# Moving five pieces of a hybrid decoder layer by a step: coupling, inversion's head, TT's second copy, the compressed weights, and the first scores' fill

## The chip, the cores and the metric

The kernel runs on one core of a Trainium2 chip. The metric is the device time of one execution in microseconds (us), as the median of several runs. Beside it stands one profiled execution, from which all the rows come.

## The reference, cut to what matters

One decoder layer with 512 tokens and a model width of 1024, in float32. A normalised stream goes through one input projection and feeds two mixers: RWKV-7 time mixing (16 heads of 64) and native sparse attention (16 heads of 64 in 4 groups; a compressed, a selected and a sliding-window branch, each a softmax). Both are gated and merged, projected and added; a gated MLP with a causal convolution of width 3 follows.

```python
def step(state, inp):                       # RWKV-7, per head, state 64 x 64
    sa = einsum('bhvk,bhk->bhv', state, a_t)
    state = state * w_t + sa[..., None] * b_t + v_t[..., None] * k_t
    return state, einsum('bhvk,bhk->bhv', state, r_t)

k_cmp = compress(kc, ...)                   # gelu(blocks of 32 tokens @ w1) @ w2
v_cmp = compress(vc, ...)
p_c = masked_softmax(q @ k_cmp - alibi); o_c = p_c @ v_cmp
o_s = softmax over the selected blocks;  o_w = softmax over the window
out = g0 * o_c + g1 * o_s + g2 * o_w

m = sigmoid(z_a) * (o_a @ w_branch_rwkv) + sigmoid(z_b) * (o_b @ w_branch_nsa)
x = x + rms_norm(m @ w_out)
x = x + rms_norm((silu(conv(h @ up_gate)) * conv(h @ up_val)) @ down)
```

## The kernel before

Each product in full precision is made of three matmuls: weights and stream are split into a high and a low part (`wh`, `wl`, `hh`, `hl`). The split of a weight block is a load on the SP queue, a cast on ACT (L124, tiles named `...h`) and a subtraction on POOL (L162, tiles named `...l`). `proj_steps` (L302 to L309) makes one block of 128 outputs in 8 steps of three matmuls (L306, L307, L308), and gives the turn away after each step. These steps are the *fill*: work that TensorE (PE) can always do, and beside which the dependent chains run.

The rest is written as generators. `drive(fill, *threads)` gives turns: in every turn each thread first advances by its rate (0.6 means three steps in five turns) and then the fill by one step. A `yield` in a generator is thus a unit of distance in the program's order. The program's order isn't yet that of the engines: a planner orders each engine's instructions when the program is built. It plays the program with modelled times and issues, on each engine, the earliest instruction of the program that it believes ready; `tc.keep_in_program_order` and `behind` (behind the last registered eviction on the same engine) pin single ones. On the chip, an engine works through its list in order and waits at an instruction whose inputs are late.

RWKV-7 is done in chunks of 64 tokens, for 8 pairs of heads in two groups of four (`GP` = 4). For each pair `p`:

- `inputs(p)`: three blocks of projections (K, R, V), 24 fill steps.
- `prep(p)`: decays and scaled keys on ACT, DVE and POOL. Its last products are `KB` and, on DVE at L576, the row block `AR`.
- `couple(p)`: copies of Dc, then some yields (L595), the turning of V on PE (`pv`, from L597) and the products of `KB` with `AR` on PE (`g`, L611), their masks on DVE (GS, L614), stores of the chunks' triangles (`ld`, `l2`, SP queue), the turning of `KB` (`pt`), its copies to BKT, the products LV and a bonus that is stored to `bvd`.

The drive of a pair runs `prep(p)` and `couple(p)` as one thread with rate `PR` = 0.6 beside the next pair's inputs as fill. In front of pair 0, `compress(kv)` makes the compressed keys (kv = 0) and values (kv = 1) as a thread of rate 0.8: 16 matmuls (`hid`), a chain for the gelu on DVE and ACT (tiles `hu`, `hv`, L416 to L427), two yields, and the last product (`kcm`; for the values at L441).

For each group, `invert` inverts the triangles of 32 x 32: loads of XL (SP queue), two yields, a copy to XP on ACT (L661), sixty operations in a row on DVE (L666, L668), then `ID` yields to the load of x1, and up to `IE` yields to a copy, two transposes and the first parts of TT. `recur`, a thread that starts `RD` = 67 turns later, makes the second triangle's block by two rounds of products (`mt`, L709; `mm`, L733) with evictions on ACT and DVE; between the rounds ACT copies the diagonal parts to TT (L722 to L724, one copy for each half of the partitions). After that come the eight chunks of the recursion, which read TT (L810) from the first on.

In the attention, `score(p8)` makes the scores of a pair of heads in 8 steps: products on PE (`s`, L1093 and L1100), a subtraction with minimum on DVE (L1107), the exponential on ACT (L1109), and the norming on DVE and POOL (L1083, L1081); `compressed(p8)` runs inside it and leaves its normed weights in `sc` (POOL, L1055). `values(p8)` has five steps, in which PE turns those weights (`turned(k)`, L140, tiles `pt`) and multiplies them with the values (`products(k)`, L1156). The compressed weights are turned to `pct` (PE, copy on ACT at L1129, low part on DVE at L1130) in the first of these steps, and read in the third:

```python
for x in range(2):
    te.matmul(acc, vcp[:, g, x, :], pct, start=x == 0, stop=False)      # L1176
```

This product opens the accumulation to which all others of the value are added. One value's steps, the next pair's scores and some fill steps (6 to 10, `FILL2`) are sorted into one order by hand. In front of value 0, `score0` runs the first scores alone with two fill steps for each of the eight; the value with index 3 (`PX`) takes what is left of this fill (`rest`) and begins with the next one, the branch products (`ub`).

Of the kernel before, what the change touches and what calls it, by code (L numbers as in the profile page):

```python
# [31 lines left out]
WS = (1, 2, 3, 3)  # L32
GP = 4
PR, CR, IY, FR = 0.6, 0.5, 31, 0.5
ID, IE, RD, RR, NG0, NQ1, PX, FN = (30, 30), (54, 54), (67, 67), (1.05, 0.85), 8, 4, 3, 1.15
NW, NU, PA, SK = 13, 3, 0.25, 4
GRP = (((0, 2), (1, 2)), ((0, 1), (0, 3)), ((0, 0),), ((1, 1), (1, 3)), ((1, 0),))
ONACT, FILL2 = (0, 2, 4, 6, 7, 8), (9, 9, 9, 6, 10, 10, 10, 10)
# [4 lines left out]
def hybrid_layer(ctx: ExitStack, tc: tile.TileContext, a, out, dbg=None, stop=None):  # L43
# [33 lines left out]
    def pz(name):  # L77
        return pzs[-1][1].tile([128, 512], F32, tag="pz", name=name, bufs=2)
# [325 lines left out]
    def compress(kv):  # L404
        w1 = cp.tile([128, 16, 128], F32, tag="w1", name=f"w1{kv}", bufs=2)
        sy.dma_start(w1, a["w1k" if kv == 0 else "w1v"])
        w2 = cp.tile([128, 64], F32, tag="w2", name=f"w2{kv}", bufs=2)
        sy.dma_start(w2, a["w2k" if kv == 0 else "w2v"])
        ph = pz(f"hid{kv}")
        for l in range(16):  # L410
            te.matmul(ph[:, 0:129], w1[:, l, :], KCs[kv][:, l % 8, l // 8:l // 8 + 129], start=l == 0, stop=l == 15)
            if l % 8 == 7:
                yield
                yield
        hb = cp.tile([128, 1], F32, tag="hb", name=f"hb{kv}", bufs=2)
        ve.tensor_copy(hb, ph[:, 0:1])  # L416
        u = cp.tile([128, 4, 32], F32, tag="hu", name=f"hu{kv}", bufs=2)
        w = cp.tile([128, 4, 32], F32, tag="hv", name=f"hv{kv}", bufs=2)
        po.memset(u, 0.0)
        ve.tensor_scalar(u[:, :, 0:NCMP], ph[:, 2:130].rearrange("p (g n) -> p g n", n=32)[:, :, 0:NCMP], hb, None,  # L420
                         op0=OP.add)
        ve.tensor_tensor(w, u, u, op=OP.mult)
        ve.tensor_scalar(w, w, 0.044715, 1.0, op0=OP.mult, op1=OP.add)
        ve.tensor_tensor(w, w, u, op=OP.mult)
        sc.activation(w, w, AF.Tanh, scale=float(np.sqrt(2.0 / np.pi)))
        ve.tensor_scalar(w, w, 0.5, 0.5, op0=OP.mult, op1=OP.add)
        ve.tensor_tensor(u, u, w, op=OP.mult)  # L427
        yield
        yield
        pm = pz(f"kcm{kv}")  # L430
        if kv == 0:
            te.matmul(pm[0:64, 0:128], w2, u.rearrange("p g n -> p (g n)"), start=True, stop=True)
            k4 = pm[0:64, 0:128].rearrange("p (g n) -> p g n", n=32)
            sc.activation(kcs[0:64, :, 0], k4, AF.Copy)
            ve.tensor_tensor(kcs[0:64, :, 1], k4, kcs[0:64, :, 0].bitcast(F32), op=OP.subtract)
            sy.dma_start(kcs[64:128].bitcast(F32), kcs[0:64].bitcast(F32))
        else:
            for e in range(2):
                es = slice(e * 32, e * 32 + 32)
                for g in range(4):  # L440
                    te.matmul(pm[es, g * 64:g * 64 + 64], u[:, g, :], w2, start=True, stop=True)  # L441
            for q in (0, 64):
                sc.activation(vcc[q:q + 64], pm[0:64, 0:256].rearrange("p (g d) -> p g d", d=64), AF.Copy)
# [143 lines left out]
    def couple(p, o, gr, i):  # L587
        R, VW, Q, EC, KB = o.R, o.VW, o.Q, o.EC, o.KB
        AR = gr.AR[i]

        if Q is not None:
            sc.activation(AR[:, 0, :], Q, AF.Copy)
        po.tensor_tensor(AR[:, 1, :].rearrange(c8, t=64), R.rearrange(c8, t=64), EC[:, :, 1:65], op=OP.mult)
        sc.activation(gr.Dc[:, i], EC[:, :, 64], AF.Copy)
        for _ in range(3 if i == GP - 1 else 2):  # L595
            yield
        for q in range(2):  # L597
            pv = px(f"pv{p}{q}")
            for j in range(4):
                c = 4 * q + j  # L600
                tr(pv[:, j * 128:(j + 1) * 128], VW[:, c * 64:c * 64 + 128], ident)
            pvv = pv.rearrange("p (c h f) -> p c h f", h=2, f=64)
            sc.activation(gr.UV[64:128, 4 * q:4 * q + 4, i], pvv[64:128], AF.Copy)
        m4 = mask.rearrange("p (s t) -> p s t", t=64)[:, None].to_broadcast([128, 4, 2, 64])
        for q in range(2):
            gh = [(pz, py)[q](f"g{p}{q}{h}") for h in range(2)]
            for j in range(4):
                c = 4 * q + j
                for h in range(2):
                    hs = slice(h * 64, (h + 1) * 64)  # L610
                    te.matmul(gh[h][:, j * 128:(j + 1) * 128], KB[hs, c].rearrange("p s t -> p (s t)"),  # L611
                              AR[hs, :, c * 64:(c + 1) * 64], start=True, stop=True)
            for h in range(2):
                ve.tensor_tensor(gr.GS[:, 0:2 + i:1 + i, 4 * q:4 * q + 4, h].rearrange("p s c t -> p c s t"),  # L614
                                 gh[h].rearrange("p (c s t) -> p c s t", s=2, t=64), m4, op=OP.mult)
            po.tensor_tensor(KB[:, 4 * q:4 * q + 4].rearrange("p c s t -> p c (s t)"),
                             KB[:, 4 * q:4 * q + 4].rearrange("p c s t -> p c (s t)"),
                             EC[:, 4 * q:4 * q + 4, 64:65].to_broadcast([128, 4, 128]), op=OP.mult)
        yield
        yield  # L620
        for b in range(2):
            bs = slice(b * 32, (b + 1) * 32)
            sy.dma_start(gr.ld[b, i].rearrange("c h i t -> i (c h) t"), gr.GS[bs, 0, :, :, bs])
        sy.dma_start(gr.l2[i].rearrange("c h i t -> i (c h) t"), gr.GS[0:32, 0, :, :, 32:64])
        yield
        yield
        pt = [px(f"pt{p}{q}") for q in range(2)]
        for q in range(2):
            for j in range(4):
                c = 4 * q + j  # L630
                m = tr(pt[q][:, j * 128:(j + 1) * 128], KB[:, c].rearrange("p s t -> p (s t)"), ident)
                if c == 0:
                    tc.keep_in_program_order(m)
            sc.activation(gr.BKT[i][:, 4 * q:4 * q + 4, :], pt[q].rearrange("p (c f) -> p c f", f=128), AF.Copy)
        pl = py(f"pl{p}")
        for c in range(8):
            for h in range(2):
                te.matmul(pl[h * 64:(h + 1) * 64, c * 64:(c + 1) * 64], gr.GS[64:128, 0, c, h, :],
                          gr.UV[64:128, c, i, h, :], start=True, stop=True)
        sc.activation(gr.LV[:, i], pl.rearrange(c8, t=64), AF.Copy)  # L640
        pbo = py(f"pbo{p}")
        te.matmul(pbo, onesr, o.rbh, start=True, stop=False)
        te.matmul(pbo, onesr, o.rbl, start=False, stop=True)
        bv = rw.tile([128, S], F32, tag="T", name=f"bv{p}", bufs=NT)
        ve.tensor_tensor(bv, pbo, VW[:, 64:], op=OP.mult)
        sy.dma_start(bvd[p], bv)
        yield
        yield

    def invert(gr, g):  # L650
        XL = rh_.tile([128, 2, 32, 32], F32, tag="XB", name=f"XL{g}", bufs=2)
        LU, XU = XL[:, 0], XL[:, 1]
        TM = rh_.tile([128, 256], F32, tag="TM", name=f"TM{g}", bufs=1)
# [40 lines left out]
    def recur(gr, g):  # L694
# [24 lines left out]
                else:  # L719
                    ve.tensor_copy(M2[up, 2 * q:2 * q + 2], ptv[up])  # L720
        evict(act_m)
        for h in range(2):  # L722
            lo = slice(64 * h, 64 * h + 32)
            behind(sc.activation(gr.diag[0][lo, :, 0:32], gr.diag[1][lo], AF.Copy))  # L724
        yield
        for q in range(GP // 2):
            pm = px(f"mm{g}{q}")
            pmv = pm.rearrange(gi, i=2, j=32)
            for i in range(2):
# [4 lines left out]
                                  stop=True)  # L734
                yield
                yield
            for h in range(2):
                lo = slice(64 * h, 64 * h + 32)
                if h == 0:
                    sc.activation(TT[lo, 2 * q:2 * q + 2, :, 32:64], pmv[lo], AF.Copy)  # L740
                else:
                    ve.tensor_copy(TT[lo, 2 * q:2 * q + 2, :, 32:64], pmv[lo])
# [378 lines left out]

    def values(p8, o):
        g = p8 // 2
        pt = pz(f"pct{p8}")
        acc = pz(f"o{p8}")
        for qb in range(4):
            tr(pt[0:64, qb * 128:(qb + 1) * 128], o.s[:, 2 * qb:2 * qb + 2].rearrange("p h n -> p (h n)"), ident)
        pct = nw.tile([128, S], F32R, tag="pct", name=f"pct{p8}", bufs=1)
        sc.activation(pct[0:64], pt[0:64], AF.Copy)  # L1129
        ve.tensor_tensor(pct[64:128], pt[0:64], pct[0:64].bitcast(F32), op=OP.subtract)  # L1130
        PTs = []

        def turned(k):
            m, parts = [], []
# [35 lines left out]
            behind_next.pop()()  # L1170
        yield
        turned(1)
        yield
        turned(2)
        for x in range(2):
# [55 lines left out]

    def score0():
        for i, _ in enumerate(score(0, os_[0])):
            for _ in range(2):
                next(fill, None)
            yield

# [361 lines left out]
```

## Time and profile before

| What | us |
|---|---|
| runs | 1161.18, 1160.72, 1158.92; median 1160.72 |
| the profiled execution | 1158.86 |
| its span | 1157.1 |
| TensorE (PE) busy | 1136.9 |
| weight loads of TensorE (PEld) busy | 912.6 |
| DVE, ACT, POOL busy | 585.2, 588.2, 555.8 |

PE's clock was granted in full (0.998 over the execution). In a row of a timeline the columns are start, length, engine, line, operation, out<-in with shapes, and in brackets how long the engine stood idle before it and what ended this. PEld is the loading of weights, which overlaps the matmuls. A matmul's end is modelled, so its length is longer than the distance to the next one. In a list of waits, PE stood at the first name until the second one's instruction was done.

### The profile page before, as it was taken

What the parts mean: (1) busy time and instruction counts of PE and PEld (TensorE: products, weight loads), DVE (VectorE), ACT (ScalarE), POOL (GpSimd) and SP (SyncE); (2) the same over time, 40 slices, a digit from 0 to 9 for tenths busy, and PEclk for the clock granted to TensorE, in tenths of its full rate; (3) what the DMA queues carried; (4) which work ended last, traced back from release to release, by engine and by line L of the source; (5) the groups of instructions that cost most, each with busy time, mean ns of one, the idle gap of its engine ahead of it and who ended that gap; (6) DMA issues with size and microseconds to landing.
All of it is one profiled execution on the core that took longest, in us unless ns stands there. A gap on an engine that the chain in (4) does not pass through costs nothing.

```text
span 1157.1 us, 19755 instructions
## 1 busy us (share of the span) xinstructions
PE 1136.9 (98%) x7338; PEld 912.6 (79%) x7338; DVE 585.2 (51%) x1194; ACT 588.2 (51%) x1158; POOL 555.8 (48%) x530
## 2 busy tenths in 40 slices
PE   9999999999999999999999999999999999999997
PEld 7888887877888787666677778889888888888886
DVE  4246655735665643677798745654333333331103
ACT  6447673544666334576676644444444444443311
POOL 4345654435765443466454425401566565564440
PEclk9999999999999999999999999999999999999999
DMA  7422345322433753125452136631233333334421
GB/s 262 108 77 80 96 108 167 103 83 64 130 107 107 201 180 111 57 81 151 145 164 67 56 108 198 221 113 47 84 99 94 98 100 93 100 100 137 127 64 73
DMA packets 95507, 131.95 MB, mean 114 GB/s; under 512 B 34033, under 2 KB 36913, under 8 KB 95154
## 3 DMA queue, kind: packets, MB, share of 16 engines
q1 hardware_dynamic: 79490, 116.26, 32.9%
q10 hardware_dynamic: 15920, 14.42, 4.1%
q8 instruction: 58, 0.95, 0.4%
q14 instruction: 39, 0.32, 0.1%
HBM read 108.30 MB, written 19.14 MB: 110 GB/s over the span
## 4 chain that ended last, share of the span: by engine, by line
PE 52%; DVE 1%; POOL 1%; issue 0%; ACT 0%; DVEq 0%; POOLq 0%; ACTq 0%
PE pu L222 6%; PE pu L223 6%; PE pu L221 6%; PE dn L1330 3%; PE dn L1329 3%; PE dn L1331 3%; PE o L1156 3%; PE ub L1213 3%; PE ub L1214 2%; PE ub L1215 2%; PE pt L140 2%; PE s L1100 1%; PE wo L1403 1%; PE wo L1401 1%; PE wo L1402 1%; PE s L1093 1%
## 5 line engine op out<-in xcount | busy, mean ns | idle before, releaser
L1109 ACT ACTIVATE p<-p,stt 128x384 f32<-128x384 f32 (+3 forms) x128 | 70.7, 554 | 33.6 <-DVE stt L1107 32.0
L1471 DVE SCALAR_TENSOR_TENSOR u<-pu,cvec,u 128x511 f32<-128x511 f32 x44 | 33.0, 750 | 101.0 <-ACT u L1470 101.0
L1107 DVE CUSTOM_DVE_ANT_0 p<-s,rh 128x384 f32<-128x384 f32 (+3 forms) x128 | 59.2, 484 | 23.6 <-PE s L1093 18.0
L1081 POOL TENSOR_SCALAR p<-p,stt 128x512 f32<-128x512 f32 (+1 forms) x64 | 38.8, 617 | 38.6 <-DVE stt L1074 25.3
L1477 DVE TENSOR_TENSOR al<-u,ah 128x512 fp32r<-128x512 f32 x22 | 23.9, 1086 | 45.5 <-ACT ah L1476 45.5
L140 PE MATMUL pt<-ident,p 128*128 128x128 f32 x320 | 44.3, 273 | 0.9 <-DVE p L1083 0.6
L1156 PE MATMUL o<-PT,vt 128*64 128x384 f32 (+3 forms) x256 | 43.0, 444 | 0.0
L140 PEld LDWEIGHTS pt<-ident,p 128*128 128x128 f32 x320 | 37.7, 141 | 5.8 <-DVE p L1083 1.1
L1475 POOL TENSOR_TENSOR u<-u,u 128x512 f32<-128x512 f32 x22 | 28.4, 1290 | 27.2 <-DVE u L1472 26.2
L1100 PE MATMUL s<-kst,qs 128*128 128x512 f32 (+1 forms) x128 | 38.2, 388 | 2.3 <-DVE stt L1107 2.2
L1470 ACT ACTIVATE u<-pu,cvec 128x512 f32<-128x512 f32 x44 | 33.6, 764 | 3.0 <-PE pu L1433 3.0
L1472 DVE SCALAR_TENSOR_TENSOR u<-pu,cvec,u 128x510 f32<-128x510 f32 x44 | 32.9, 749 | 1.6
L1083 DVE TENSOR_SCALAR p<-p,stt 128x512 f32<-128x512 f32 (+1 forms) x64 | 32.6, 538 | 0.8
L1156 PEld LDWEIGHTS o<-PT,vt 128*64 128x64 f32 x256 | 16.6, 136 | 19.3 <-issue 17.4
L1147 ACT ACTIVATE PT<-pt 128x512 f32<-128x512 f32 x48 | 27.5, 585 | 7.8 <-PE pt L140 7.7
L1100 PEld LDWEIGHTS s<-kst,qs 128*128 128x128 f32 x128 | 21.5, 189 | 10.0 <-DVE stt L1107 5.2
L1377 DVE TENSOR_TENSOR p2ss<-p2ss 128x1 f32<-128x1 f32 x4 | 0.6, 160 | 52.1 <-ACT p2jl L1375 52.1
L1149 DVE COPY PT<-pt 128x512 f32<-128x512 f32 x32 | 21.6, 675 | 8.3 <-PE pt L140 8.3
L1476 ACT ACTIVATE ah<-u 128x512 fp32r<-128x512 f32 x22 | 13.9, 633 | 22.0 <-POOL u L1475 22.0
L1109 ACT ACTIVATION_READ_ACCUMULATOR p<-p,stt 128x1 f32 x128 | 24.1, 188 | 0.0
L815 ACT ACTIVATE UV<-xs 64x256 f32<-64x256 f32 x16 | 6.0, 378 | 35.0 <-PE xs L810 34.6
L668 DVE TENSOR_TENSOR XP<-XP,TM 128x30 f32<-128x30 f32 (+14 forms) x60 | 20.3, 338 | 2.0
(1760 smaller groups left out, 3936.4 us busy)
## 6 DMA issues: line engine op xcount, KB each, us to landing
gtd<-gt ACTq DMA_DIRECT2D x16, 256.0 KB, 2.3
qs<-qd SPq DMA_DIRECT2D x32, 128.0 KB, 3.2
g<-gtd SPq DMA_DIRECT2D x16, 256.0 KB, 2.9
xt<-in_x_dram SPq DMA_DIRECT2D x4, 512.0 KB, 5.7
bvd<-bv SPq DMA_DIRECT2D x8, 256.0 KB, 2.4
bvl<-bvd SPq DMA_DIRECT2D x8, 256.0 KB, 3.0
kst<-kst ACTq DMA_DIRECT2D x16, 128.0 KB, 2.3
t<-oad SPq DMA_DIRECT2D x8, 256.0 KB, 3.1
```

Of the source, the lines that this page charges most:

```text
L140: return te.transpose(o, i, ident)
L221: te.matmul(p, wh(k), mh(k), start=first and k == 0, stop=False)
L222: te.matmul(p, wh(k), ml(k), start=False, stop=False)
L223: te.matmul(p, wl(k), mh(k), start=False, stop=last and k == n - 1)
L1081: po.tensor_scalar(o.pe[e, b, k], o.pe[e, b, k], w, 1.0, op0=OP.mult, op1=OP.mult)
L1100: m = te.matmul(s_[:, :n], qt, kt[:, x, b, :n], start=x == 0, stop=x == 1)
L1107: ve.tensor_tensor_reduce(sb, parts[b], rh[e][:, (3 - qb) * 128:], -1.0, BIG, OP.add, OP.min, st[e][:, 0, i:i + 1])
L1109: sc.activation(sb, sb, AF.Exp, scale=-1.0, bias=st[e][:, 0, i:i + 1], accum_out=st[e][:, 1, i:i + 1])
L1156: te.matmul(acc[e * 64:e * 64 + 64, j * 128:], vt[:, j, b * 256 + g * 64:b * 256 + g * 64 + 64], m[e][:, c:c + n], start=False, stop=k == ...
L1213: te.matmul(p, wh(k), sh[:, k, :], start=k == 0, stop=False)
L1329: te.matmul(acc[half, t], sh[:, k, tsl], wh[kk], start=k == 0, stop=False)
L1330: te.matmul(acc[half, t], sh[:, k, tsl], wl[kk], start=False, stop=False)
```

## The change

It moves instructions in the program's order and removes none.

- `ID` and `IE` go from 30 and 54 to 29 and 53, and `invert` gives one turn away before its first load: loads, copy and the DVE chain are one step later, what follows stays in its turn.
- `compress`: three yields instead of two ahead of the last product for kv = 0, two as before for kv = 1.
- `couple`: three yields ahead of `pv` and `g` for all pairs but 0, 4 and 5. Before, pairs 3 and 7 had three and all others two.
- `recur`: the copy of the diagonal's second half is issued after the first round-half of the second products instead of with the first copy.
- `values`: the turning of the compressed weights moves from the first step to the second.
- `score0`: three fill steps instead of two after each of the last two scores.

```diff
-ID, IE, RD, RR, NG0, NQ1, PX, FN = (30, 30), (54, 54), (67, 67), (1.05, 0.85), 8, 4, 3, 1.15
+ID, IE, RD, RR, NG0, NQ1, PX, FN = (29, 29), (53, 53), (67, 67), (1.05, 0.85), 8, 4, 3, 1.15
...
         ve.tensor_tensor(u, u, w, op=OP.mult)
-        yield
-        yield
+        for _ in range(3 - kv):
+            yield
         pm = pz(f"kcm{kv}")
...
         sc.activation(gr.Dc[:, i], EC[:, :, 64], AF.Copy)
-        for _ in range(3 if i == GP - 1 else 2):
+        for _ in range(2 if p in (0, GP, GP + 1) else 3):
             yield
...
     def invert(gr, g):
+        yield
         XL = rh_.tile([128, 2, 32, 32], F32, tag="XB", name=f"XL{g}", bufs=2)
...
         evict(act_m)
-        for h in range(2):
+
+        def diag(h):
             lo = slice(64 * h, 64 * h + 32)
             behind(sc.activation(gr.diag[0][lo, :, 0:32], gr.diag[1][lo], AF.Copy))
+
+        diag(0)
         yield
...
                 yield
                 yield
+            if q == 0:
+                diag(1)
             for h in range(2):
                 lo = slice(64 * h, 64 * h + 32)
...
     def values(p8, o):
         g = p8 // 2
-        pt = pz(f"pct{p8}")
         acc = pz(f"o{p8}")
-        for qb in range(4):
-            tr(pt[0:64, qb * 128:(qb + 1) * 128], o.s[:, 2 * qb:2 * qb + 2].rearrange("p h n -> p (h n)"), ident)
-        pct = nw.tile([128, S], F32R, tag="pct", name=f"pct{p8}", bufs=1)
-        sc.activation(pct[0:64], pt[0:64], AF.Copy)
-        ve.tensor_tensor(pct[64:128], pt[0:64], pct[0:64].bitcast(F32), op=OP.subtract)
         PTs = []
+
+        def compressed_turned():
+            pt = pz(f"pct{p8}")
...
+            return pct
...
         yield
         turned(1)
+        pct = compressed_turned()
         yield
         turned(2)
...
         for i, _ in enumerate(score(0, os_[0])):
-            for _ in range(2):
+            for _ in range(2 + (i > 5)):
                 next(fill, None)
             yield
```

More of the change, by code (lines that the diff above doesn't have):

```diff
@@ L1123, in values @@
         g = p8 // 2
-        pt = pz(f"pct{p8}")
         acc = pz(f"o{p8}")
-        for qb in range(4):
-            tr(pt[0:64, qb * 128:(qb + 1) * 128], o.s[:, 2 * qb:2 * qb + 2].rearrange("p h n -> p (h n)"), ident)
-        pct = nw.tile([128, S], F32R, tag="pct", name=f"pct{p8}", bufs=1)
-        sc.activation(pct[0:64], pt[0:64], AF.Copy)
-        ve.tensor_tensor(pct[64:128], pt[0:64], pct[0:64].bitcast(F32), op=OP.subtract)
-        PTs = []
+        PTs = []
+        def compressed_turned():
+            pt = pz(f"pct{p8}")
+            for qb in range(4):
+                tr(pt[0:64, qb * 128:(qb + 1) * 128], o.s[:, 2 * qb:2 * qb + 2].rearrange("p h n -> p (h n)"), ident)
+            pct = nw.tile([128, S], F32R, tag="pct", name=f"pct{p8}", bufs=1)
+            sc.activation(pct[0:64], pt[0:64], AF.Copy)
+            ve.tensor_tensor(pct[64:128], pt[0:64], pct[0:64].bitcast(F32), op=OP.subtract)
+            return pct
         def turned(k):
```

## The prediction

> **What bounds the kernel now.** I read three views: the page for the busy shares, the list of waits of TensorE (PE) for the places where it stops, and the timelines around each place that the diff touches.
>
> ```profile
> span 1157.1 us, 19755 instructions
> ...
> PE 1136.9 (98%) x7338; PEld 912.6 (79%) x7338; DVE 585.2 (51%) x1194; ACT 588.2 (51%) x1158; POOL 555.8 (48%) x530
> ```
>
> PE is busy for 1136.9 of 1157.1 us. The change removes no instruction, so it can only win back part of the 20.2 us in which PE stands still, or add to them. The waits name most of these:
>
> ```profile
> PE s L1100 <- DVE stt L1107: 2.2, 4, 1.2
> PE g L611 <- DVE AR L576: 1.8, 3, 0.6
> PE warm L116 <- DVE zero L111: 1.6, 1, 1.6
> PE pg L887 <- DVE stt L1074: 1.3, 1, 1.3
> PE q L308 <- POOL q5l L162: 0.9, 1, 0.9
> PE n1p L140 <- DVE n1xn L198: 0.8, 1, 0.8
> PE pct L140 <- POOL sc L1055: 0.8, 1, 0.8
> PE gt L308 <- POOL gt05l L162: 0.7, 1, 0.7
> PE pg L887 <- DVE stt L1107: 0.7, 1, 0.7
> PE gt L308 <- POOL gt17l L162: 0.6, 1, 0.6
> PE pt L140 <- DVE p L1083: 0.6, 1, 0.6
> PE pct L140 <- DVE stt L1074: 0.6, 1, 0.6
> PE kcm L441 <- DVE hu L427: 0.4, 1, 0.4
> PE gt L308 <- POOL gt02l L162: 0.3, 1, 0.3
> ```
>
> The columns are total us, times, longest. Six of these rows belong to lines that the diff moves: g (1.8), pct twice (0.8 and 0.6), kcm (0.4), gt05 (0.7, behind the TT copies, as shown below), gt17 and gt02 (0.6 and 0.3, behind the inversion's head). They add up to 5.2 us. That is nearly all that this change can win, about 0.45% of the time. A kernel of this kind can be told from no change at about 0.2%, 2.3 us.
>
> **Part by part.** The engines' orders come from a planner that issues what it believes ready, in program order among those. An added `yield` therefore moves an instruction behind some more fill work on PE; it doesn't move a ready time.
>
> *Coupling.* Five pairs have three yields afterwards, but pairs 3 and 7 had three already: only pairs 1, 2 and 6 move. Exactly three g waits exist. Pair 1:
>
> ```profile
> 113.36 0.39 PE L307 MATMUL r<-hl,r2h 128*128 128x512 f32 x1
> 113.59 0.39 PE L308 MATMUL r<-hh,r2l 128*128 128x512 f32 x1
> 113.82 1.03 PE L140 MATMUL pv<-ident,V 128*128 128x128 f32 x8
> 115.46 0.94 PE L611 MATMUL g<-AR,KB 64*128 64x128 f32 x12 [0.60 <-DVE AR L576]
> ```
>
> Fill matmuls start 0.23 us apart, so a fill step of three is 0.68 us. The coupling runs at 0.6 steps per fill step, so one yield is 1/0.6 = 1.67 fill steps or 1.1 us of PE work ahead of pv and g. That covers 0.60 with 0.5 to spare. Pair 3, which has the extra yield already, shows the result:
>
> ```profile
> 163.24 0.68 DVE L576 SCALAR_TENSOR_TENSOR AR<-Q,pb 128x512 f32<-128x512 f32 x1
> ...
> 164.32 0.38 PE L611 MATMUL g<-AR,KB 64*128 64x128 f32 x2
> ```
>
> AR ends at 163.92 and g starts 0.40 later, with no wait. The term is 3 x 0.60 = 1.8 us; its bounds are 0 (the planner keeps its order) and 1.8. With g, everything behind it in `couple` moves 0.5 us later in time (1.1 of work less 0.6 of wait): the masks on DVE, the scaling of KB on POOL, the two ld stores and the l2 store and the bvd store on SP with the weight loads queued behind them, the BKT and LV copies on ACT. None of the three is a group's last pair, whose stores the inversion reads, so nobody waits for these stores. Prep plus coupling is now 15 calls at 0.6, 26 turns against 25 of the fill, and the last two calls issue nothing; so the fill still covers it. If the tail delayed the next prep by more than the 0.40 of pair 3, a wait would come back there; I cost it at nothing.
>
> *Compression.* `3 - kv` adds a yield to kv = 0, but the kcm wait sits at kv = 1:
>
> ```profile
> L424 DVE TENSOR_TENSOR hv<-hv,hu x2: 292/858/1424, 61.5 to 71.2; 128x128 f32<-128x128 f32 x2
> ...
> 71.15 1.29 POOL L162 TENSOR_TENSOR v0l<-v01r,v0h 128x512 fp32r<-128x512 f32 x1 [2.63 <-ACT v0h L124]
> 71.17 1.42 DVE L424 TENSOR_TENSOR hv<-hv,hu 128x128 f32<-128x128 f32 x1
> ```
>
> The second kv's whole chain moves one step (0.68 us) with its matmul, so the distance between them stays. What can change is the company: the same product took 0.29 us alone and 1.42 us beside POOL's subtraction. If it misses POOL, the chain is 1.1 us shorter and the wait of 0.4 goes; if it meets it again, nothing changes. I take 0.2, the middle, as no row shows the new company; bounds 0 and 0.4. The Trainium skill (SBUF — State Buffer, "Who interferes with whom") says that a DVE instruction with two SBUF inputs contends with a POOL instruction that reads SBUF, and that the later one blocks until the other ends. This trace agrees (POOL ends at 72.44, the product at 72.59). By that rule, one step later the square, two operations ahead, would be blocked instead until the same 72.44; my estimate, with two short operations (0.29 us each, as the lone product) still to come after it, is a chain that ends 0.6 us later before a matmul that is due 0.68 us later: 0.1 won, a sum of 3.5. Without that rule, the 1.42 us being the product's own, the term is 0 and the sum 3.4.
>
> *TT's second copy.* On ACT:
>
> ```profile
> 234.25 4.05 ACT L724 ACTIVATE TT<-XL 32x1024 f32<-32x1024 f32 x2
> 238.32 0.63 ACT L124 ACTIVATE gt05h<-gt050r 128x512 fp32r<-128x512 f32 x1
> ```
>
> The two copies hold ACT for 4.05 us; gt05's first cast follows at once, POOL's low part after it, and PE waits 0.7. With the second copy issued after the first half of the second products, and behind the last eviction (gt14's, at the block's end), gt05's two casts go 2.0 us earlier. The wait goes: 0.7, bounds 0 and 0.7. The copy (2.0 us) then follows gt14's eviction. Behind it wait v0's casts and the second TT eviction; v0's products and the first TT product, the copy's reader, come after gt05's eight steps (8 x 0.68 = 5.4 us), so the cover is 3 us; without it the copy would cost its 2.0. In group 1 no PE wait stands beside the copies, so nothing there.
>
> *Inversion's head.* ACT, group 0:
>
> ```profile
> 181.96 1.03 ACT L661 ACTIVATE XP<-XL 128x1024 f32<-128x1024 f32 x1 [0.53 <-ACT gt L477]
> 182.93 0.61 ACT L124 ACTIVATE gt02h<-gt021r 128x512 fp32r<-128x512 f32 x1
> ```
>
> If the cast went ahead of the 1.03 us copy, gt02's 0.3 and gt17's 0.6 would go. But the copy is issued in the third turn and now in the fourth, the block with that cast only in the ninth; both still start when their data are there. So 0, with 0.9 as the upper end. The lower end: the sixty dependent DVE operations start a step (0.68 us) later; ID and IE take it back for what comes after, so only the copy to XU can be late, and the recursion's thread comes in turns that don't move. If PE met it anyway, 2 x 0.7.
>
> *Compressed weights.* The pct transposes leave the first step of `values`, where they wait for sc (0.8 and 0.6), for the second. These waits are in a stage where DVE is full:
>
> ```profile
> 478.00:493.00 15.00, 13.41 (x83) 9.45 (x79) 13.75 (x50) 12.38 (x36) 9.16 (x13) 1.00 0.27 92
> ```
>
> (Columns: length, then PE, PEld, DVE, ACT, POOL busy.) DVE is busy 13.75 of 15 us, so what PE does next also waits for DVE soon: I count half, 0.7, between 0 and 1.4. The price is a new race, from the transposes to the product that reads them (value 4):
>
> ```profile
> 598.13 0.60 PE L140 MATMUL pct<-ident,sc 128*64 128x128 f32 x4
> ...
> 600.08 0.68 DVE L1130 TENSOR_TENSOR pct<-pct,pct 64x512 fp32r<-64x512 f32 x1
> ...
> 605.03 0.71 PE L140 MATMUL pt<-ident,p 128*128 128x128 f32 x5
> ...
> 609.44 0.71 PE L1176 MATMUL o<-pct,vcp 128*128 128x512 f32 x2
> ```
>
> The chain over ACT and DVE takes 600.76 - 598.13 = 2.6 us; it used to have 11. It would start where the second turn ends (605.74), and the product comes at 609.44 plus about 0.4 for the transposes inserted before it: 4.1 us, 1.5 to spare. Queued behind the product on PE are the products of the first two turns. I take 0.3 for one or two values that are late. Net 0.4.
>
> *score0.* Two fill steps, 2 x 0.68 = 1.4 us of PE work, come into the stage above, where PE idles 1.59 of 15 us, and are missing in the value with index 3. Bounds +1.4 (idle filled, not missed later) and -1.4. The new block needs a bank whose eviction is queued on the full DVE and ACT, so I take 0.5.
>
> *Sum.* 1.8 + 0.2 + 0.7 + 0 + 0.4 + 0.5 = 3.6 us. The profiled execution took 1158.86 us, 1.9 below the median of the runs (1160.72). 1158.86 - 3.6 = 1155.3; on the median, 1157.1, which I predict.
>
> **Rivals.**
> 1. *The planner makes little of it.* It plays times that differ from the chip's by some tenths, as the g waits show; moved steps re-deal hundreds of later choices, and new waits of 0.3 to 0.9, like q5's, replace old ones. For it: the stage after 478 is bound by DVE, not by order. Against: the g waits lie outside it, three times the same. Only about 1 us remains: 1159.7.
> 2. *More than I count.* The casts pass the inversion's copy (+0.9), all of the pct and kcm waits go (+0.9): 5.4 us, 1155.3. For it: ACT waits 0.53 us ahead of the inversion's copy (row above), time in which a ready cast could go.
> 3. *Slower: pct is late.* At the second products of each of eight values. It decides from a chain of 4.1 us instead of 2.6: then each further us is paid eight times. Four more instructions of the size of the ACT casts above (0.6 us) in front of it make 5.0: 8 x 0.9 = 7.2 lost, 3.2 won by the other parts: 1164.7. Against: ACT is not full in the later values, and the planner fills a wait that it foresees.
>
> **Chances.** Forecast 0.43 (1155.5 to 1158.4), rival 1 0.26 (1158.4 to 1161.5), rival 2 0.19 (1153.5 to 1155.5), rival 3 0.12. Faster by over 0.2% is forecast and rival 2, 0.62; within is rival 1, 0.26; slower 0.12. The range takes in all but rival 3: 1153.5 to 1161.5.
>
> **What would show it.** In the waits: the row of g gone (right) or three of 0.6 still there; gt05l gone; gt02l and gt17l still there; kcm smaller. In ACT's timeline: gt05's casts between the two TT copies. A row of o, L1176, waiting for pct or L1130 would be rival 3; new rows of q, ub or s in the values with index 0 to 3 that make up for the old, rival 1. I am wrong if PE's idle time falls by less than 2 us or more than 5.

## The result, and the profile after

The changed kernel takes 1153.75 us in the median (1153.59 to 1155.63) against 1160.72 (1158.92 to 1161.18): ratio 0.995, 95% interval 0.9937 to 0.9962, so faster by 0.4 to 0.6%. The profiled execution took 1155.63 us. (The change has six parts, one more than the title counts: the compression.) First its page, then the waits of TensorE (PE): total us, times, longest.

```profile
span 1153.8 us, 19761 instructions
...
PE 1139.2 (99%) x7338; PEld 914.0 (79%) x7338; DVE 582.1 (50%) x1194; ACT 588.3 (51%) x1158; POOL 556.0 (48%) x530
```

```profile
PE warm L116 <- DVE zero L111: 1.6, 1, 1.6
PE s L1106 <- DVE stt L1113: 1.6, 5, 0.6
PE pg L893 <- DVE stt L1079: 1.0, 1, 1.0
PE pg L893 <- DVE stt L1113: 0.7, 2, 0.4
PE q L308 <- POOL q5l L162: 0.7, 1, 0.7
PE pt L140 <- DVE p L1089: 0.6, 1, 0.6
PE gt L308 <- POOL gt17l L162: 0.6, 1, 0.6
PE pct L140 <- DVE stt L1080: 0.6, 1, 0.6
PE gt L308 <- POOL gt02l L162: 0.4, 1, 0.4
...
```

The rows of g (1.8), gt05l (0.7), kcm (0.4) and one of the two of pct (0.8) are gone. Those behind the inversion's head (gt17l, gt02l) stand as before, and no row names pct as what a product waits for. PE's idle time, span less busy, falls from 20.2 to 14.6 us; 0.8 of these 5.6 us lie ahead of the first projection (2.42 us idle there before, 1.59 after), in the part described next.

The two profiled executions can't be subtracted as they are: they differ in the first 15 us, which the change doesn't touch. The first projection (L241) starts at 12.89 us before and at 14.50 after, and the same four small matmuls of L119 take 1.99 us in the one and 3.78 in the other. First before, then after:

```profile
5.30 1.99 PE L119 MATMUL gb<-g1r 1*128 1x512 f32 x4
...
12.89 0.68 PE L241 MATMUL b<-hh,b0h 128*128 128x256 f32 x1
```

```profile
5.30 3.78 PE L119 MATMUL gb<-g1r 1*128 1x512 f32 x4
...
14.50 0.68 PE L241 MATMUL b<-hh,b0h 128*128 128x256 f32 x1
```

In the fourteen profiled executions of this study that start lies between 12.44 and 14.85 us, whatever the kernel: four times at 12.44 to 12.89, ten times at 14.08 to 14.85. The runs of a kernel lie mostly on two levels some 2 us apart, and where there are several runs the profiled one lies on the level of its start. So the working goes by stages, from one first matmul on PE to another: kc (the start of the compression's inputs), gt00 (the fill of the first inversion), q4 and ub06 (first and last part of the scores and values). Their starts in the two timelines, before first:

```profile
32.21 0.40 PE L306 MATMUL kc<-hh,kc00h 128*128 128x512 f32 x1
...
151.79 0.39 PE L306 MATMUL gt<-hh,gt00h 128*128 128x512 f32 x1
...
445.95 0.50 PE L306 MATMUL q<-hh,q4h 128*128 128x512 f32 x1
...
689.57 0.40 PE L1213 MATMUL ub<-hh,wb06h 128*128 128x512 f32 x1
```

```profile
33.78 0.40 PE L306 MATMUL kc<-hh,kc00h 128*128 128x512 f32 x1
...
152.13 0.39 PE L306 MATMUL gt<-hh,gt00h 128*128 128x512 f32 x1
...
444.61 0.50 PE L306 MATMUL q<-hh,q4h 128*128 128x512 f32 x1
...
686.34 0.40 PE L1223 MATMUL ub<-hh,wb06h 128*128 128x512 f32 x1
```

The differences, with those of every kernel below (from the same four rows of each timeline):

| Kernel | kc to gt00 | gt00 to q4 | q4 to ub06 |
|---|---|---|---|
| before | 119.58 | 294.16 | 243.62 |
| the change | 118.35 | 292.48 | 241.73 |
| coupling alone | 118.76 | 293.69 | 243.50 |
| TT's second copy alone | 119.59 | 292.94 | 243.48 |
| compressed weights alone | 119.60 | 294.22 | 244.48 |
| score0's fill alone | 119.87 | 294.09 | 244.55 |
| weights and fill | 119.57 | 294.11 | 241.69 |
| compression alone | 119.17 | 294.19 | 243.57 |
| the change, head held behind a cast | 118.29 | 290.62 | 241.76 |
| the change, a third late fill step | 118.30 | 292.46 | 243.10 |
| weights late from value 1 on | 119.58 | 294.14 | 247.94 |
| weights late in value 0 only | 119.62 | 294.16 | 244.84 |
| head held, weights late from value 1 | 118.30 | 290.59 | 241.95 |
| weights alone, five idle matmuls | 119.59 | 294.13 | 243.78 |

Where an edit touches nothing in a stage, the stage repeats within some 0.1 us in nearly all rows (0.3 in the first row of the fill alone, where a wait of 0.3 us for the keys' `kcm` stands that no other run has), so tenths can be read here that the whole time hides. The change wins 1.23 + 1.68 + 1.89 = 4.8 us. Its parts, tried by themselves below, add up to this: coupling and compression 0.82 + 0.41 in the first stage, coupling and TT's copy 0.47 + 1.22 in the second, and the two attention parts together 1.93 in the third. What comes behind ub06 takes 467.53 us before and 467.46 after (467.46 to 468.05 over all kernels).

### The profile page after: what moved, and what is told of

It is laid out like the page before. It is cut to its first block, busy times and chain, and to the rows that moved or that the text cites. A ratio compares the mean times of both kernels' runs of the same rounds, so it can differ in the third digit from the quotient of the medians.

```text
span 1153.8 us, 19761 instructions
## 1 busy us (share of the span) xinstructions
PE 1139.2 (99%) x7338; PEld 914.0 (79%) x7338; DVE 582.1 (50%) x1194; ACT 588.3 (51%) x1158; POOL 556.0 (48%) x530
## 4 chain that ended last, share of the span: by engine, by line
PE 50%; DVE 2%; POOL 0%; ACT 0%; issue 0%; DVEq 0%; POOLq 0%; ACTq 0%
PE pu L222 6%; PE pu L223 6%; PE pu L221 6%; PE dn L1340 3%; PE dn L1339 3%; PE dn L1341 3%; PE o L1165 3%; PE ub L1223 3%; PE ub L1225 2%; PE ub L1224 2%; PE pt L140 2%; PE wo L1411 1%; PE wo L1412 1%; PE wo L1413 1%; PE s L1106 1%; PE s L1099 1%
```

## The experiments

**Coupling alone**: before, with the one line

```diff
-        for _ in range(3 if i == GP - 1 else 2):
+        for _ in range(2 if p in (0, GP, GP + 1) else 3):
```

> The kernel before with the coupling's extra yield alone (pairs 1, 2 and 6). Measured from the first projection matmul (b, L241) to the end, which leaves out the start of the execution: 1144.2 us before, 1139.3 with the whole change. Theory (each part closes its own waits): the g row of the waits goes, 1.8 us in 3 places; nothing else moves; 1142.4. Rival (the planner deals the later choices anew, gains don't belong to a part): the score stage, q4's first matmul to ub02's, 179.4 us before, changes by more than 0.3 us although no line of it is touched.

Measured: 1158.46 us, ratio 0.9985 (0.9976 to 0.9995). The g row is gone, and the first two stages win 0.82 + 0.47 = 1.3 us, not 1.8. The waits themselves were worth more than their rows: from the last pv to the first g it took 0.87 us and now 0.20, so 0.67 each. What is given back stands in the list of PEld's waits, here that of the changed kernel; before has no such row:

```profile
PEld v L306 <- issue: 1.2, 3, 0.4
```

Three times, after each of the moved couplings, the next pair's V block now starts late: from the last r matmul to the first of v and from there to the second it takes 0.38 + 0.31 us instead of 0.23 + 0.23, so 0.23 lost. 3 x (0.67 - 0.23) = 1.3. "Issue" names no releaser; why v starts late was not settled.

**TT's second copy alone**: `diag(1)` behind the first half of the second products, nothing else.

```diff
-        for h in range(2):
+
+        def diag(h):
             lo = slice(64 * h, 64 * h + 32)
             behind(sc.activation(gr.diag[0][lo, :, 0:32], gr.diag[1][lo], AF.Copy))
+
+        diag(0)
         yield
...
+            if q == 0:
+                diag(1)
```

> The kernel before with TT's second copy behind the second products alone. Theory: gt05l's wait goes and with it 0.7 to 1.3 us between gt03's first matmul and the first TT product (37.1 us before, 35.8 with the whole change), so that stage is 35.8 here too and all others stay within 0.1: 1142.9 from the first projection matmul to the end. Rival (part of that stage's 1.3 us comes from the inversion's head or the coupling): the stage is 36.4 or more.

Measured: 1158.77 us, ratio 0.999 (0.998 to 0.9999). The gt05l row is gone and gt00 to q4 wins 1.2 us, for a row of 0.68. Before, PE's timeline:

```profile
238.57 0.39 PE L308 MATMUL gt<-hh,gt14l 128*128 128x512 f32 x1
239.01 0.50 PE L306 MATMUL gt<-hh,gt05h 128*128 128x512 f32 x1
239.34 0.40 PE L307 MATMUL gt<-hl,gt05h 128*128 128x512 f32 x1
240.42 0.50 PE L308 MATMUL gt<-hh,gt05l 128*128 128x512 f32 x1 [0.68 <-POOL gt05l L162]
240.85 0.69 PE L733 MATMUL mm<-TT,x 32*32 32x32 f32 x32
```

Starts of such matmuls are 0.23 us apart where nothing waits. Here they are 0.44 (a short wait for the cast, which has no row), 0.33 (the restart), 1.08 (the wait) and 0.43 (against 0.32 elsewhere ahead of such a mm): 0.21 + 0.10 + 0.85 + 0.11 = 1.27. A row of the waits counts from a matmul's modelled end, 0.39 us after its start, and leaves out what the stop costs on either side.

**Compressed weights alone**: `compressed_turned()` (the change's function) behind `turned(1)`, and no turning in the first step, as in the change.

```diff
         turned(1)
+        pct = compressed_turned()
         yield
```

> The kernel before with the compressed weights turned in the second step of the values alone. The score stage, q4's first matmul to ub06's, takes 243.6 us before and 241.7 with the whole change. Theory of the prediction (half of the pct waits, less a late product or two): 0.4 less, 243.2. Rival A (pct is the whole of the 1.9): 241.7. Rival B (the fill steps are): 243.6 or more, the pct wait of value 1 gone and others in its place.

Measured: 1161.03 us, ratio 1.0011 (1.0001 to 1.002); alone it loses, and its stage takes 244.48 us. PE's timeline at value 0, then two windows (length; PE, PEld, DVE, ACT, POOL busy; then PE's granted clock):

```profile
509.09 0.66 PE L140 MATMUL pt<-ident,p 128*128 128x128 f32 x4 [1.04 <-ACT PT L1150]
509.92 0.66 PE L140 MATMUL pt<-ident,p 128*128 128x128 f32 x4 [0.18 <-DVE PT L1152]
511.51 1.22 PE L1180 MATMUL o<-pct,vcp 128*128 128x512 f32 x2 [0.93 <-DVE pct L1133]
512.66 2.94 PE L1159 MATMUL o<-PT,vt 128*64 128x256 f32 x16
515.53 0.41 PE L140 MATMUL pct<-ident,sc 128*64 128x128 f32 x2
```

```profile
507.89:511.30 3.41, 1.47 (x9) 0.84 (x8) 2.90 (x5) 3.28 (x8) 2.26 (x3) 1.00 0.17 38
511.30:514.71 3.41, 3.20 (x12) 1.75 (x14) 2.49 (x8) 2.85 (x10) 2.27 (x3) 0.50 0.00 0
```

Late pct is waited for, in this one value (the prediction's rival 3). But the larger part seems to be the clock: after 3.41 us in which PE was busy for only 1.47, it was granted half its clock for the next 3.41 us. The product of pct and the sixteen behind it took 515.53 - 511.51 = 4.02 us; in "weights and fill" below, at full clock, 2.54. So the half clock cost these matmuls some 1.5 us; without it the stage would by this estimate have won about 0.6, which no run shows by itself. ACT's order shows why pct was late: ACT stood 1.66 us for DVE, with the copies of PT and pct behind it.

```profile
507.99 0.42 ACT L1046 ACTIVATE sc<-sc 128x256 f32<-128x256 f32 x1 [1.66 <-DVE stt L1074]
508.44 0.60 ACT L1150 ACTIVATE PT<-pt 128x512 f32<-128x512 f32 x1
508.93 0.58 ACT L1132 ACTIVATE pct<-pct 64x512 fp32r<-64x512 f32 x1
```

**score0's fill alone**:

```diff
-            for _ in range(2):
+            for _ in range(2 + (i > 5)):
```

> The kernel before with the two extra fill steps in score0 alone. The score stage, q4's first matmul to ub06's, takes 243.6 us before and 241.7 with the whole change. Theory of the prediction: 0.5 less, 243.1, the fill's blocks kwp1 and q5 a few us earlier. Rival B (these steps are the whole gain): 241.7. Rival A (pct is): 243.6 or more, with the work missing in the value with index 3.

Measured: 1159.99 us, ratio 1.0008 (0.9998 to 1.0017). The stage grew by 0.93 us at a full clock. The rows of pg fell (2.0 to 1.3), but s waits in six places instead of four (2.3 us), and a new row of s, for y, has 0.6. The waits are not the loss: PE's idle time in the stage even fell, from 7.60 to 6.87 us, while the same matmuls kept it busy for 1.66 us longer (237.68 against 236.02). By the starts in PE's timeline, PE goes from a product of PT straight to a fill matmul 20 times instead of 16, and each such change costs 0.1 to 0.2 us more than the plain distance (the fill's second matmul alone starts 0.34 us behind its first instead of 0.23). This would be 0.4 to 0.8 us; no run tried it alone, "weights and fill", which wins, has 18 such changes, and the rest is open.

**Weights and fill together**: the two diffs above in one kernel.

> Before with the two attention parts alone: the compressed weights turned in the second step, and three fill steps after each of the last two first scores. Alone each of them made the stage from q4's first matmul to ub06's longer (243.62 before, 244.47 and 244.55 us), and in the changed kernel, which has both, it takes 241.73. Theory (the two make the gain together, as the order of this stage is dealt anew by both): the stage takes 241.7, within 0.2, and the time falls by 1.9 us against before, ratio 0.9984. Rival (the prices add up, and the gain comes from another part, upstream): 245.4 and 1.8 us slower.

Measured: 1157.68 us, ratio 0.9986 (0.9976 to 0.9995); the stage takes 241.69, as in the whole change (241.73). The two make the gain, 1.9 us, though their prices alone are +0.86 and +0.93: they don't add. PE's idle time in the stage falls from 7.60 to 5.88 us. At value 0 nothing waits now:

```profile
508.36 1.04 PE L140 MATMUL pt<-ident,p 128*128 128x128 f32 x8
509.35 0.74 PE L1180 MATMUL o<-pct,vcp 128*128 128x512 f32 x2
510.01 1.95 PE L1159 MATMUL o<-PT,vt 128*64 128x256 f32 x16
511.89 0.30 PE L140 MATMUL pct<-ident,sc 128*64 128x128 f32 x1
```

pct's copy on ACT starts at 506.55, 59.3 us behind q4's first matmul (447.23), where it started 61.6 behind it (508.93, 447.35) with the weights alone: with the fill brought forward the engines' lists are in another order there, and ACT has no such stop for DVE.

**Compression alone**:

```diff
-        yield
-        yield
+        for _ in range(3 - kv):
+            yield
```

> Before with the compression's edit alone: three yields for the keys and two for the values. From kc's first matmul to gt00's before takes 119.58 us, the changed kernel 118.34, and the coupling alone 118.75. Theory (the product misses the one on POOL, and the kcm wait goes): 119.2, without a kcm row among the waits. Rival (the 0.4 comes from the coupling and the compression together, or from the pieces of order around them): 119.6, with the kcm row at 0.3 to 0.4.

Measured: 1160.03 us in one run; 119.17 against 119.58, so 0.41, and the row is gone. The product that took 1.42 us takes 0.29, as no POOL instruction runs beside it any more (POOL's ends at 72.27, the next starts at 75.44); DVE, then POOL, of this kernel:

```profile
73.41 0.29 DVE L424 TENSOR_TENSOR hv<-hv,hu 128x128 f32<-128x128 f32 x1
```

```profile
71.00 1.27 POOL L162 TENSOR_TENSOR v0l<-v01r,v0h 128x512 fp32r<-128x512 f32 x1
75.44 1.27 POOL L162 TENSOR_TENSOR k1l<-k10r,k1h 128x512 fp32r<-128x512 f32 x1 [3.17 <-ACT k1h L124]
```

**The head held behind a cast**: the changed kernel with

```diff
-ID, IE, RD, RR, NG0, NQ1, PX, FN = (29, 29), (53, 53), (67, 67), (1.05, 0.85), 8, 4, 3, 1.15
+ID, IE, RD, RR, NG0, NQ1, PX, FN = (23, 23), (47, 47), (67, 67), (1.05, 0.85), 8, 4, 3, 1.15
...
-        yield
+        for _ in range(7):
+            yield
...
-        sc.activation(XP.rearrange("u i c -> u c i"), LU, AF.Copy)
+        tc.keep_in_program_order(sc.activation(XP.rearrange("u i c -> u c i"), LU, AF.Copy))
```

> The changed kernel, with the inversion's head seven steps later instead of one (ID and IE down by as much) and its copy to XP held behind what the program puts ahead of it, so that on ACT the casts of gt02 and gt17 come ahead of that copy. Theory (these two waits stand behind the 1.03 us copy, and the DVE chain of the inversion has time to spare): both rows gone, 1.0 us less from the first b matmul to the end (1138.3 against 1139.33), about 1152.8 in the median. Rival (the chain, begun 1 us later or more, ends late for the copy to XU or the first round of mt): the rows are gone, and a new wait of XU's readers or of mt gives back 0.5 to 2 us; no gain or a loss.

Measured: 1153.9 us, ratio to before 0.9948 (0.9933 to 0.9963). Both rows are gone, and gt00 to q4 takes 290.62 against 292.48: 1.86 us for rows of 0.4 and 0.6, nearly twice the 1.0 that was expected, and nothing given back. ACT, in this kernel:

```profile
180.21 0.63 ACT L124 ACTIVATE gt02h<-gt021r 128x512 fp32r<-128x512 f32 x1 [0.46 <-ACT gt L477]
180.75 1.01 ACT L663 ACTIVATE XP<-XL 128x1024 f32<-128x1024 f32 x1
```

Its median lies no lower than the changed kernel's. But the runs of both lie on two levels: 1151.83 and three at 1153.86 to 1154.15 here, three at 1153.59 to 1153.75 and two at 1155.42 and 1155.63 there. Level by level it is 1.5 to 1.8 us faster, about what the stages say. The profiled runs, 1151.83 here and 1155.63 there, have the early and the late start; for the others the level is inferred from the time.

**A third late fill step**: the changed kernel with `i > 4` in the place of `i > 5`.

> The changed kernel with a third fill step after each of the last three first scores instead of the last two. Theory (what the last fill step wins depends on how the planner's order happens to fall out, not on the amount of work brought forward): the stage from q4's first matmul to ub06's moves by 0.5 to 3 us against 241.73, most likely up (242.5 to 244.5). Rival (each step brought forward fills idle time of PE): 241.4 to 241.7, or less.

Measured: 1156.86 us in one run; the stage takes 243.10. One more step brought forward costs 1.4 us. So not each step brought forward fills idle time of PE; that the order's falling out decides is what is left, not what one run shows.

**Weights late from value 1 on**, and **in value 0 only**: before, with the weights turned late in the values that the condition leaves over; for the second kernel it is `p8 > 0`. The function is the change's.

```diff
+        pct = compressed_turned() if p8 == 0 else None
         turned(0)
...
         turned(1)
+        if pct is None:
+            pct = compressed_turned()
```

> Before with the late turning of the compressed weights in the values with index 1 to 7; in value 0 they are turned in the first step, as before. With all eight turned late and nothing else changed, PE waited three times in a row at value 0 (1.2, 0.3 and 1.0 us), and the granted clock stood at 0.50 from 511.3 to 514.6. Theory (the late turning wins some 0.8 us in the later values, and alone it lost because the waits at value 0 let the clock fall, some 1.7 us): no stretch at 0.50 in this stage, and from q4's first matmul to ub06's 242.8 us, within 0.4 (243.62 before, 244.48 with all eight late). Rival (the clock is only a part, and the order dealt anew costs by itself): 243.6 or more at a full clock.

> Before with the late turning in value 0 alone, the other seven as before. Theory (value 0's row of waits and the clock that falls behind it are the whole price): a stretch of some 3 us at a granted clock of 0.50 near 512, and the stage takes 244.5 to 245.5 us. Rival (the place of the waits is dealt anew, and the clock falls only by chance): no such stretch, 243.0 to 244.2.

Measured: 1164.62 us, ratio 1.0034 (1.0019 to 1.0048), for the first; 1159.87 in one run for the second. The first fell outside both theories: 247.94 us in the stage, with two stretches at half clock, at value 0 and, behind a wait of 1.9 us for the pg products, near 546. Two stretches at half clock can cost half of 6.8, 3.4 us, at most, so some 0.9 of its 4.3 or more come from something else, the order by what is left. The second behaved as the theory said in its time (244.84), but over two windows in a row. First the windows of "from value 1 on", then those of "value 0 only":

```profile
508.61:512.02 3.41, 1.80 (x10) 1.33 (x10) 3.10 (x8) 2.28 (x6) 1.93 (x3) 1.00 0.17 38
512.02:515.43 3.41, 3.41 (x17) 1.83 (x16) 2.57 (x8) 3.38 (x12) 2.16 (x4) 0.50 0.00 0
542.74:546.15 3.41, 1.55 (x9) 1.20 (x9) 2.86 (x12) 1.75 (x9) 3.19 (x4) 1.00 0.55 159
546.15:549.56 3.41, 3.41 (x12) 1.51 (x12) 2.97 (x5) 1.54 (x5) 2.15 (x3) 0.50 0.21 77
```

```profile
504.09:507.50 3.41, 1.41 (x6) 0.77 (x6) 3.08 (x10) 1.73 (x5) 1.16 (x2) 1.00 0.53 141
507.50:510.91 3.41, 2.94 (x10) 1.77 (x10) 2.75 (x8) 3.41 (x11) 1.45 (x3) 0.50 0.01 3
510.91:514.32 3.41, 3.41 (x17) 1.72 (x16) 2.12 (x4) 1.56 (x6) 2.96 (x4) 0.50 0.00 0
```

So value 0 is not the only place: a re-dealing brought about a halving at another place as well.

**The head held, weights late from value 1 on**: the two edits on the changed kernel.

> The changed kernel with the inversion's head seven steps later and its copy held behind gt02's cast (1.7 us less from the first b matmul to the end than the changed kernel), and beside it the late turning from value 1 on only. Theory (with value 0's chain as early as before, the waits at value 0 are shorter and no later value loses): the stage from q4's first matmul to ub06's takes 241.0 to 241.7 (241.76 with all eight late), so 0 to 0.7 less in all, about 1151.5 us. Rival (the planner's order is dealt anew and the gain of the two parts together is lost): 242.5 to 244.5, 1153 us or more.

Measured: 1153.82 us, ratio to before 0.9946 (0.9931 to 0.9961); the stage takes 241.95, between the two expectations and 0.2 above the kernel with all eight late. No gain, and no stretch at half clock: the fill of score0 is in it.

**Weights alone, with five idle matmuls** in value 0, kept in program order between `turned(2)` and the product of pct:

```diff
+        def busy(n):
+            for _ in range(n if p8 == 0 else 0):
+                tc.keep_in_program_order(te.matmul(acc, vcp[:, g, 0, :], hh[:, 0, :], start=True, stop=True))
...
         turned(2)
+        busy(5)
```

> Before with all eight values' compressed weights turned late (the part that alone cost 0.85 us in its stage), and five more matmuls of 0.23 us in value 0, which write what the product of pct overwrites: work without use, put where PE waits 1.09 us for pct. It is told by the clock's records that every stretch at 0.50 lasts 3.41 us, or twice that, and stands behind 3.41 us in which PE was busy for 1.41 to 1.80 us; no stretch stands behind 1.94 us or more. Theory (the lost clock is the price): PE is busy some 2.4 us of the 3.41 now, the clock stays at 1.00, and from the first of the pg products (506.87) to the first pct transpose of the next value (515.53) it takes 7.1 us instead of 8.66, though PE has 1.15 us more to do; the stage takes 242.9, within 0.5. Rival (the clock falls for another reason than PE's idleness, or the late pct itself is the price): 8.66 us or more there, 244.5 or more in the stage.

Measured: 1159.51 us, ratio 1.0 (0.999 to 1.001), the stage 243.78. The clock fell all the same, 2 us earlier, from 509.09 us on, while the added matmuls begin only at 510.95, so they could not keep it up:

```profile
505.68:509.09 3.41, 1.63 (x7) 0.71 (x5) 2.77 (x9) 1.70 (x5) 0.82 (x1) 1.00 0.49 132
509.09:512.50 3.41, 3.17 (x12) 2.76 (x13) 2.75 (x8) 3.41 (x11) 1.45 (x4) 0.50 0.10 22
```

The half clock now lay over eight transposes and most of the useless matmuls, and the product of pct with the sixteen behind it had the full one: 515.34 - 512.90 = 2.44 us instead of 4.02. With more work in it, the stage is 0.7 us shorter. The expectation missed: the clock was to stay at 1.00 and the stage to take 242.9 (within 0.5). The distance that was to be 7.1 us can't be read as it was meant, since the next transposes of pct come 8 us later in this order; from the first pg product to the end of the sixteen it is 515.34 - 507.11 = 8.23. So the run doesn't show that the half clock alone was the price: pct's wait is hidden, too, and the two effects were not parted. What stands is the price of the half clock for the same eighteen matmuls, 4.02 us against 2.44 and 2.54.

## Why the prediction was right, and where its steps were off

The direction was right, and so was the mechanism for the coupling, TT's copy and the head, and for the compression as one of two cases; it was not for the attention parts. The size was low, 3.6 us forecast and 4.8 by stages.

The median, 1153.75, lies inside the stated range but in rival 2's part of it (1153.5 to 1155.5), not in the forecast's own (1155.5 to 1158.4). The 7.0 us between the medians are not all the change's: before's median lies on the upper of its two levels and the changed kernel's on the lower, and level by level it is 5.3 (1158.92 against 1153.6 to 1153.75, and 1160.6 to 1161.2 against 1155.4 to 1155.6).

PE's idle time fell by 5.6 us, more than the 5 that was to show the prediction wrong, but 0.8 of this is the start's; from the first projection on it fell by 4.8. The 5.2 us of rows (seven of them, not six) that were taken for nearly all there is to win are no bound: the head held behind a cast wins 1.9 more than the change's 4.8.

Part by part:

- *Coupling*, 1.8: measured 1.3. The three waits went as said, and their true price was 0.67 each; what was missed is that v's start gives back 0.23 of each. The prediction looked for what the later tail would cost in the next prep, and put that at nothing.
- *Compression*, 0.2: 0.41, the upper bound. The product missed POOL (0.29 us), so the 1.42 us were not its own length, and the later meeting didn't come about either, for which the prediction's estimate by the Trainium skill (SBUF — State Buffer, "Who interferes with whom") was 0.1. Counted from kc's first matmul (32.21 before, 33.77 here), the product came 0.68 us later, one step, as forecast; but POOL's subtraction came 1.7 us earlier (38.94 and 37.23), as did its cast on ACT. The prediction had left POOL where it was; that the two would miss each other was one of its cases, and luck.
- *TT's second copy*, 0.7 as an upper bound: 1.2 to 1.27. The bound was no bound, since a row of the waits isn't the whole price of a stop. That this half us too little and the coupling's half us too much cancel is luck.
- *Inversion's head*, 0: right, the two rows stand. The upper end of 0.9 was mis-sized in the same way: with the cast truly ahead of the copy it is 1.86.
- *Compressed weights and score0*, 0.4 and 0.5 as two terms: 1.9 together, and +0.86 and +0.93 alone. The sum is what failed: I priced each against the old order, and each changes the order that the other meets. Each term alone had the wrong sign, and nothing in the prediction gave the gain of the two together, so that this half of the sum came out positive is luck. The race that I feared (rival 3) is real, once, in value 0 and without the fill, where I had read it at value 4; with the fill the chain is early enough. A fall of the clock was not in the prediction at all.

Rival 2 gave a time near the result (1155.3), but mostly for other reasons than its own: the kcm row and one of the two pct rows went, but the casts did not pass the inversion's copy.

## What to carry to other kernels

Read a wait of PE from the starts of the matmuls around it, not from its row: here rows of 0.4 to 0.7 us were worth 0.41 to 1.27 where nothing was given back. Compare two executions by stages between named first matmuls, so that a start that varies by 2 us doesn't stand in the sum. And don't add up edits to one stage whose order a planner deals: try them together and singly, and look at the granted clock wherever several waits stand within some 3 us.

## What the hardware showed that was not expected

PE's clock halves in the middle of a kernel without any long stop. Between the first 15 us and the last few (every trace ends at half clock), each stretch at half clock lasted 3.41 us, or twice that, and began at a fixed beat: the two of "from value 1 on" begin 546.15 - 512.02 = 34.13 us apart, ten times 3.413, and in each trace the clock's record changes a whole number of such windows after the clock was first raised (with the weights alone at 12.96 and 511.30 us, 146 x 3.4133). Counted in these windows, PE was busy for 1.41 to 1.80 us in those ahead of a halving (1.41, 1.47, 1.55, 1.63, 1.80), with no single stop over 2 us. Every other window at full clock between 15 and 1140 us kept it, and none of them has less than 1.81 us; the emptiest is one of before's own (its clock was raised at 12.17, and 145 windows later comes 507.10):

```profile
507.10:510.51 3.41, 1.81 (x11) 1.35 (x11) 3.09 (x8) 2.29 (x6) 1.94 (x3) 1.00 0.17 38
```

So the edge lies near 1.8 us of the 3.41, some 53%; the hundredth between the two sides can't be trusted, as ends of matmuls are modelled. Before stands right at this edge, and the emptiest window of the changed kernel has 2.31. The place of the beat counts as well: the kernel with TT's second copy alone had 1.79 us in 3.41 and kept its clock, since this stretch lies across two windows, and none of its windows has less than 2.07:

```profile
507.40:510.81 3.41, 1.79 (x10) 1.19 (x9) 3.24 (x8) 2.13 (x5) 1.78 (x3) 1.00 0.17 39
505.91:509.32 3.41, 2.07 (x10) 1.43 (x9) 2.25 (x9) 1.03 (x4) 0.29 (x1) 1.00 0.27 62
```

To come back to full clock took more: behind a halved window with 2.94 us busy ("value 0 only") the clock stayed at half, behind those with 3.17 us and more it rose.

The Trainium skill (TensorE: Matmul & The Clock Gate, "Part 1: The HAM clock gate") gives a free-running window of 3413 ns, and half rate after an idle one. Length and beat agree with these traces; a window did not have to be idle, 41 to 53% busy was little enough, and there the measurement decides. The same page says that the place of the window in a run makes the number of slow matmuls at the start vary. The traces agree: in the four with the early start a window at full clock begins between 4.81 and 5.75 us (before at 5.34, when the four matmuls of L119 begin, which then take 1.99 us), in the ten others the first one that is recorded begins between 12.96 and 14.55 (the changed kernel at 13.82; its four take 3.78). The place was observed here, not set.
